# Short reads ahead of the loads, a re-scheduled head and earlier next tiles in an RMSNorm and QKV projection

## The chip, the core and the metric

The kernel runs on one core of a Trainium2 chip. The metric is the time of one execution on the device in microseconds (us); lower is better. A core has five engines with an instruction stream each: TensorE (PE, matmuls), VectorE (DVE), ScalarE (ACT), GpSimd (POOL) and SyncE (SP, which only issues transfers here). Sixteen DMA engines carry out the transfers that SP and ACT issue.

## The reference

```python
def setup_inputs():
    batch, n_heads, seq, head_dim = 8, 12, 1024, 64
    dim = n_heads * head_dim
    # x (8, 1024, 768) randn, gamma (768) ones, w_qkv (768, 2304) randn * 0.1, eps 1e-5

def reference(x, gamma, w_qkv, eps):
    rms = np.sqrt(np.mean(x ** 2, axis=-1, keepdims=True) + eps)
    x_norm = x / rms * gamma
    return np.matmul(x_norm, w_qkv).astype(np.float32)
```

There are 8,192 rows of 768 numbers. Each row is divided by its root mean square, scaled by gamma and multiplied with a 768 x 2304 matrix.

## The kernel before, in words

Rows are taken in 64 tiles of 128. A tile x_t is loaded as f32 (384 KB), cast to bf16 and transposed to xT, so that its 768 columns stand in 6 K blocks of 128 along the partitions. The weights are multiplied by gamma and converted to bf16 once (`conv`), into w_b, and stay on the chip. A tile's output has column groups at 0, 512, 1024, 1536 (512 wide) and 2048 (256 wide). Each group is six matmuls, one for each K block, into one PSUM bank (`mm`, L216). The row's factor 1/rms is applied when the bank is emptied (`evac`, L230 on DVE, L232 on ACT). Two groups of 512 make one store of 512 KB; the last group makes one of 128 KB (L236).

Everything is put in order by hand. Each step is entered in a list with a due time, the list is sorted, and the steps are issued in that order; every engine then works through its own steps in order. The due times only order the steps; nothing waits for the clock.

The head treats the first six tiles together with the weights. The weights come in 11 pieces (`PIECES`: K blocks from and to, first column, width), and `ARRIVALS` gives the order of x tiles and pieces on SP's queue: x0 x1 x2, three weight blocks, x3, and so on. Tiles 0 to 2 are transposed on TensorE directly in f32, in two halves ("trA" and "trB", L197, copied by "cpA" and "cpB"); tiles 3 to 5 are cast first and transposed in bf16 (L183). `HEAD_PLAN` lists what each engine does: conversions of weight blocks on DVE, ACT or POOL, matmuls by tile, column and K blocks, evacuations. TensorE starts with 30 matmuls on zeros (`idle`, L265) and does 5 more after tile 2's transposes. Gamma is loaded by ACT's queue (L122) and transposed on TensorE (L247).

From tile 6 on there is a steady loop with the due time `now` of the tile's first matmul. The load of x is due 15 us before, the cast 8.5, a DMA transpose on SP's queue (`trans_dma`, L206) 7.5, the square sum (`stat`) 5 and the reciprocal 3. A tile's matmuls take 5.83 us in this list. All x loads, weight loads, stores and DMA transposes go through SP in the listed order. The framework gives DMAs eight completion semaphores in turn, and a DMA waits for the one issued eight before it.

Pools set how many buffers there are: eight for x_t, four for the bf16 cast xb, nine for xT, seven for each kind of output tile, eight PSUM banks.

Of the kernel before, what the change touches and what calls it, by code (L numbers as in the profile page):

```python
# [7 lines left out]

ARRIVALS = "xxxwwwxwwwwwxxwww"
PIECES = [(0, 1, 0, 512), (1, 2, 0, 512), (2, 3, 0, 512), (3, 4, 0, 512), (4, 5, 0, 512), (5, 6, 0, 512), (0, 3, 512, 512), (3, 6, 512, 512), (0, 6, 1024, 512), (0, 6, 1536, 512), (0, 6, 2048, 256)]

EARLY = 3


HEAD_PLAN = [
    (4.41, "trA", 0), (4.45, "stat", 0), (5.28, "trB", 0), (5.42, "cpA", 0, "DVE"),
    (5.71, "trA", 1), (5.85, "cpB", 0, "ACT"), (6.10, "recip", 0), (6.44, "stat", 2),
    (6.59, "trB", 1), (6.73, "cpA", 1, "DVE"), (6.80, "trA", 2), (7.11, "conv", 0, 0, "POOL"),  # L20
    (7.24, "trB", 2), (7.41, "cpB", 1, "DVE"), (7.77, "cpA", 2, "ACT"),
    (7.81, "conv", 1, 1, "DVE"), (8.02, "mm", 0, 0, "0"), (8.23, "mm", 1, 0, "0"),
    (8.29, "recip", 2), (8.39, "cpB", 2, "ACT"), (8.45, "conv", 2, 2, "DVE"),
    (8.45, "mm", 2, 0, "0"), (8.66, "mm", 0, 0, "1"), (8.75, "stat", 1), (8.88, "mm", 1, 0, "1"),
    (9.10, "mm", 2, 0, "1"), (9.31, "mm", 0, 0, "2"), (9.44, "cast", 3, "DVE"),
    (9.53, "mm", 1, 0, "2"), (9.74, "mm", 2, 0, "2"), (10.05, "tr", 3), (10.08, "stat", 3),
    (10.11, "conv", 3, 3, "DVE"), (10.59, "recip", 1), (10.65, "mm", 0, 0, "3"),
    (10.78, "conv", 4, 4, "DVE"), (10.87, "mm", 1, 0, "3"), (11.09, "mm", 2, 0, "3"),
    (11.26, "cp", 3, "DVE"), (11.32, "mm", 0, 0, "4"), (11.45, "conv", 5, 5, "ACT"),
    (11.54, "mm", 1, 0, "4"), (11.76, "mm", 2, 0, "4"), (11.82, "recip", 3),  # L30
    (11.97, "mm", 3, 0, "01234"), (13.05, "mm", 0, 0, "5"), (13.27, "mm", 1, 0, "5"),
    (13.47, "conv", 6, 0, "DVE"), (13.47, "conv", 6, 1, "ACT"), (13.47, "conv", 6, 2, "POOL"),
    (13.48, "mm", 2, 0, "5"), (13.70, "mm", 3, 0, "5"), (13.95, "evac", 2, 0, "DVE"),
    (14.01, "mm", 0, 512, "0"), (14.18, "evac", 0, 0, "ACT"), (14.22, "mm", 1, 512, "0"),
    (14.44, "mm", 0, 512, "12"), (14.70, "evac", 1, 0, "DVE"), (14.87, "evac", 3, 0, "ACT"),
    (14.87, "mm", 1, 512, "12"), (15.30, "mm", 2, 512, "012"), (15.48, "conv", 7, 4, "DVE"),
    (15.48, "conv", 7, 5, "POOL"), (15.95, "mm", 3, 512, "012"), (16.33, "conv", 7, 3, "POOL"),
    (16.47, "cast", 4, "DVE"), (16.47, "stat", 4), (16.60, "mm", 0, 512, "45"),
    (17.03, "mm", 1, 512, "4"), (17.24, "tr", 4), (17.47, "cast", 5, "DVE"),
    (17.58, "mm", 0, 512, "3"), (17.79, "mm", 1, 512, "35"), (17.80, "stat", 5),  # L40
    (18.02, "cp", 4, "DVE"), (18.23, "tr", 5), (18.56, "mm", 2, 512, "345"), (18.58, "recip", 4),
    (18.74, "evac", 1, 512, "DVE"), (19.13, "evac", 0, 512, "ACT"), (19.21, "mm", 3, 512, "345"),
    (19.49, "evac", 2, 512, "DVE"), (19.86, "mm", 4, 0, "012345"), (20.02, "evac", 3, 512, "ACT"),
    (20.24, "recip", 5), (20.40, "cp", 5, "DVE"), (21.15, "mm", 4, 512, "012345"),
    (21.49, "conv", 8, 2, "DVE"), (21.49, "conv", 8, 3, "ACT"), (21.97, "conv", 8, 0, "DVE"),
    (22.20, "conv", 8, 4, "ACT"), (22.45, "mm", 5, 0, "012345"), (22.45, "evac", 4, 0, "DVE"),
    (22.91, "evac", 4, 512, "ACT"), (23.60, "conv", 8, 1, "ACT"), (23.74, "mm", 5, 512, "012345"),
    (23.90, "evac", 5, 0, "DVE"), (24.31, "conv", 8, 5, "ACT"), (25.04, "mm", 0, 1024, "012345"),
    (25.20, "evac", 5, 512, "DVE"), (25.51, "conv", 9, 0, "POOL"), (25.51, "conv", 9, 1, "ACT"),
    (25.95, "conv", 9, 5, "DVE"), (26.33, "mm", 1, 1024, "012345"), (26.43, "conv", 9, 4, "DVE"),  # L50
    (26.49, "evac", 0, 1024, "ACT"), (26.91, "conv", 9, 2, "DVE"), (27.39, "conv", 9, 3, "DVE"),
    (27.63, "mm", 2, 1024, "012345"), (27.87, "evac", 1, 1024, "DVE"),
    (27.90, "conv", 10, 0, "POOL"), (27.90, "conv", 10, 2, "ACT"), (28.38, "conv", 10, 3, "ACT"),
    (28.62, "conv", 10, 5, "DVE"), (28.86, "conv", 10, 4, "ACT"), (28.92, "conv", 10, 1, "DVE"),
    (28.92, "mm", 3, 1024, "012345"), (29.22, "evac", 2, 1024, "DVE"),
    (30.22, "mm", 4, 1024, "012345"), (30.38, "evac", 3, 1024, "DVE"),
    (31.51, "mm", 5, 1024, "012345"), (31.67, "evac", 4, 1024, "DVE"),
    (32.81, "mm", 0, 1536, "012345"), (32.97, "evac", 5, 1024, "DVE"),
    (34.10, "mm", 1, 1536, "012345"), (34.26, "evac", 0, 1536, "DVE"),
    (35.39, "mm", 2, 1536, "012345"), (35.55, "evac", 1, 1536, "DVE"),  # L60
    (36.69, "mm", 3, 1536, "012345"), (36.85, "evac", 2, 1536, "DVE"),
    (37.98, "mm", 4, 1536, "012345"), (38.14, "evac", 3, 1536, "DVE"),
    (39.28, "mm", 5, 1536, "012345"), (39.44, "evac", 4, 1536, "DVE"),
    (40.57, "mm", 0, 2048, "012345"), (40.73, "evac", 5, 1536, "DVE"),
    (41.23, "mm", 1, 2048, "012345"), (41.39, "evac", 0, 2048, "ACT"),
    (41.88, "mm", 2, 2048, "012345"), (42.04, "evac", 1, 2048, "DVE"),
    (42.54, "mm", 3, 2048, "012345"), (42.70, "evac", 2, 2048, "DVE"),
    (43.19, "mm", 4, 2048, "012345"), (43.35, "evac", 3, 2048, "DVE"),
    (43.85, "mm", 5, 2048, "012345"), (44.01, "evac", 4, 2048, "DVE"),
    (44.67, "evac", 5, 2048, "DVE"),  # L70
]
HEAD_END = 44.51


@with_exitstack
def kernel(
# [8 lines left out]
    nc = tc.nc  # L85
    f32 = mybir.dt.float32
# [4 lines left out]
    xf = x.flatten_outer_dims()  # L91
    of = out.flatten_outer_dims()
    M, K = xf.shape
# [3 lines left out]
    KO = K // P  # L97
    MT = M // P
    NT = 512
    HEAD = ARRIVALS.count("x")  # L100
    inv_k = 1.0 / float(K)
    PIECE_BUFS = {(k1 - k0, n): sum((q[1] - q[0], q[3]) == (k1 - k0, n) for q in PIECES)
                  for k0, k1, _, n in PIECES}

    PARTS = [(0, 1024), (1024, 1024), (2048, N - 2048)]

    singles = ctx.enter_context(tc.tile_pool(name="singles", bufs=1))
    wst = ctx.enter_context(tc.tile_pool(name="wst", bufs=3))
    xin = ctx.enter_context(tc.tile_pool(name="xin", bufs=8))
    stats = ctx.enter_context(tc.tile_pool(name="stats", bufs=12))  # L110
    junk = ctx.enter_context(tc.tile_pool(name="junk", bufs=2))
    xbp = ctx.enter_context(tc.tile_pool(name="xbp", bufs=4))
    xTp = ctx.enter_context(tc.tile_pool(name="xTp", bufs=HEAD + 3))
    outp = ctx.enter_context(tc.tile_pool(name="outp", bufs=7))
    psum = ctx.enter_context(tc.tile_pool(name="psum", bufs=8, space=bass.MemoryType.PSUM))

# [1 line left out]

    warm = singles.tile([P, P], bf16)
    nc.vector.memset(warm, 0.0)  # L120
    g6 = singles.tile([KO, P], f32)
    nc.scalar.dma_start(out=g6, in_=gamma.rearrange("(ko p) -> ko p", p=P))  # L122
    eps_sb = singles.tile([P, 1], f32)
# [77 lines left out]
            XT[t] = xTp.tile([P, KO, P], bf16, name="xT")  # L201
        copy(eng, XT[t][:, slice(*HALF[h]), :], PT[t, h])

    def trans_dma(t):
        XT[t] = xTp.tile([P, KO, P], bf16, name="xT")
        nc.sync.dma_start_transpose(out=XT[t], in_=XB[t])  # L206

    begun = {}

# [32 lines left out]
    def at(time, fn, *args):  # L242
        plan.append((time, len(plan), fn, args))
# [8 lines left out]
    def evac_at(time, t, n0, eng, gap):  # L252
        at(time, evac, t, n0, eng)
        h = part(n0)
        nl = min(NT, N - n0)
        left[t, h] = left.get((t, h), PARTS[h][1]) - nl
        if t == MT - 1:
            at(time + gap - 0.5, store, t, h, n0, nl)
        elif left[t, h] == 0:
            at(time + gap, store, t, h, *PARTS[h])  # L260
# [4 lines left out]
            nc.tensor.matmul(out=wps, lhsT=warm, rhs=warm, start=True, stop=True)  # L265


    nx = nw = 0
    for n, kind in enumerate(ARRIVALS):
        if kind == "x":  # L270
            at(0.1 * n - 9, load_x, nx)
            nx += 1
        else:
            at(0.1 * n - 9, load_w, nw)
            nw += 1
    at(0.0, idle, 30)
    ops = {"conv": conv, "cast": cast, "stat": stat, "recip": recip, "tr": tr, "cp": cp, "mm": mm}
    for time, op, *args in HEAD_PLAN:
        if op == "evac":
            evac_at(time, *args, gap=1.0)  # L280
        elif op[-1] in "AB":
            at(time, tr_half if op[:2] == "tr" else cp_half, args[0], op[-1], *args[1:])
        else:
            if op == "mm":
                args[2] = [int(k) for k in args[2]]
            at(time, ops[op], *args)
        if op == "trA" and args[0] == 0:
            at(time + 0.1, gamma_in)
        if op == "trB" and args[0] == EARLY - 1:
            at(time + 0.1, idle, 5)  # L290


    US = 6 * 0.2158 / 512
    now, flip = HEAD_END, 0
    for t in range(HEAD, MT):
        at(now - 15, load_x, t)
        at(now - 8.5, cast, t)
        at(now - 7.5, trans_dma, t)
        at(now - 5, stat, t)
        at(now - 3, recip, t)  # L300
        for n0 in range(0, N, NT):
            at(now, mm, t, n0, range(KO))
            now += min(NT, N - n0) * US
            flip ^= 1
            evac_at(now + 0.2, t, n0, "DVE" if flip else "ACT", gap=1.2)
# [38 lines left out]
```

## Time and profile before

| what | value |
|---|---|
| median of 4 runs | 390.05 us (389.92 to 390.29) |
| the profiled execution's own time | 389.57 us |
| its span, first to last instruction | 387.8 us |
| first matmul of the kernel proper | 8.52 us |
| TensorE busy | 381.9 us (98%) |
| HBM read, written | 32.25 MB, 75.50 MB |
| load of an x tile, issue to landing, median | 4.3 us |
| DMA transpose, issue to landing, median | 4.4 us |

The span runs from the first to the last instruction in the profile; the time of an execution also holds what lies around it. Engines are named as above; PEld is the loading of the stationary operand, which overlaps PE. In a timeline line the first number is the start, the second the duration in us, then engine, line, operation, output and inputs, shapes and count; brackets give how long the engine had been idle and what released it. The chain of waits is followed back from the last instruction, each step to what released it. Line numbers are those of the kernel before.

### The profile page before, as it was taken

To read this page: it belongs to the slowest core of one execution; us is meant where nothing else is said; L and a number is where in the kernel's file an instruction comes from. 1 tells how busy PE (TensorE), PEld (TensorE's weight loads), DVE (VectorE), ACT (ScalarE), POOL (GpSimd) and SP (SyncE) were. 2 spreads that over 40 slices of the span, in tenths; PEclk is the share of its full clock that TensorE was granted. 3 is DMA by queue.
4 is the path that set the end of the run, shared out by engine and by line. 5 is a ranking of instruction groups with operands and counts; after the bars stand their busy time and mean duration, and the time that the engine had idled before them with its cause. 6 is when DMAs were issued, how large, how long until landed. Compare 5 with 4: busy or idle time off the path is not lost.

```text
span 387.8 us, 5539 instructions
## 1 busy us (share of the span) xinstructions
PE 381.9 (98%) x1992; PEld 194.4 (50%) x1992; DVE 159.3 (41%) x317; ACT 178.3 (46%) x359; POOL 5.9 (2%) x12
## 2 busy tenths in 40 slices
PE   7999999999999999999999999999999999999996
PEld 6444644554554554554554554554554554554553
DVE  3676634343433343433343333343334343333332
ACT  6662244444444544444534444534434535434532
POOL 1310000000000000000000000000000000000000
PEclk9999999999999999999999999999999999999999
DMA  7999999999999999999999999999999999999974
GB/s 282 393 385 350 315 353 284 369 337 288 292 341 302 299 303 299 275 350 302 285 319 297 300 314 289 315 319 299 279 329 302 290 327 284 289 333 292 311 246 189
DMA packets 87606, 119.51 MB, mean 308 GB/s; under 512 B 50710, under 2 KB 59676, under 8 KB 87580
## 3 DMA queue, kind: packets, MB, share of 16 engines
q1 hardware_dynamic: 87568, 119.17, 100.8%
q8 instruction: 15, 0.25, 0.3%
q14 instruction: 11, 0.09, 0.1%
q10 hardware_dynamic: 12, 0.00, 0.0%
HBM read 32.25 MB, written 75.50 MB: 278 GB/s over the span
## 4 chain that ended last, share of the span: by engine, by line
PE 95%; DMA 3%; SPq 1%; DVE 0%; issue 0%; ACT 0%
PE pm L216 94%; DMA w_f<-in_w_qkv_dram 2%; DMA xT<-xb 1%; SPq L140 0%; SPq L145 0%; PE pm L183 0%; DVE w_b L151 0%; ACT ot L232 0%; DVE ot L230 0%
## 5 line engine op out<-in xcount | busy, mean ns | idle before, releaser
L216 PE MATMUL pm<-w_b,xT 128*128 128x512 bf16 (+1 forms) x1920 | 374.5, 358 | 1.3 <-POOL w_b L155 1.0
L216 PEld LDWEIGHTS <-xT 128*128 128x128 bf16 x1920 | 187.6, 98 | 187.1 <-issue 1.5
L230 DVE TENSOR_SCALAR ot<-pm,rstd 128x512 f32<-128x512 f32 (+1 forms) x168 | 116.9, 697 | 211.5 <-PE pm L216 211.4
L232 ACT ACTIVATE ot<-pm,rstd 128x512 f32<-128x512 f32 (+1 forms) x152 | 98.0, 645 | 187.3 <-PE pm L216 142.0
L170 ACT ACTIVATE sq<-x_t 128x768 bf16<-128x768 f32 x64 | 53.4, 835 | 10.0 <-DMA x_t<-in_x_dram 10.0
L159 DVE CAST xb<-x_t 128x768 bf16<-128x768 f32 x61 | 33.1, 543 | 3.6 <-DMA x_t<-in_x_dram 3.6
L172 ACT ACTIVATE rms<-ssq,eps_sb 128x1 f32<-128x1 f32 x64 | 18.9, 295 | 2.1
L170 ACT ACTIVATION_READ_ACCUMULATOR sq<-x_t 128x1 f32 x64 | 12.3, 192 | 0.0
L177 DVE RECIPROCAL rstd<-rms 128x1 f32<-128x1 f32 x64 | 9.8, 153 | 0.0
L153 ACT ACTIVATE w_b<-w_f,g_sb 128x512 bf16<-128x512 f32 (+1 forms) x10 | 6.1, 651 | 5.3 <-DMA w_f<-in_w_qkv_dram 5.3
L151 DVE TENSOR_SCALAR w_b<-w_f,g_sb 128x512 bf16<-128x512 f32 (+1 forms) x14 | 6.5, 494 | 4.9 <-DMA w_f<-in_w_qkv_dram 4.6
L155 POOL TENSOR_SCALAR w_b<-w_f,g_sb 128x512 bf16<-128x512 f32 (+1 forms) x6 | 5.2, 867 | 23.0 <-DMA w_f<-in_w_qkv_dram 23.0
L265 PE MATMUL pm<-warm 128*128 128x128 bf16 x35 | 3.8, 300 | 1.0 <-DVE eps_sb L124 1.0
L265 PEld LDWEIGHTS <-warm 128*128 128x128 bf16 x35 | 3.5, 142 | 1.0 <-DVE eps_sb L124 1.0
L197 PE MATMUL pm<-ident_f,x_t 128*128 128x128 f32 x18 | 3.0, 309 | 0.0
L197 PEld LDWEIGHTS pm<-ident_f,x_t 128*128 128x128 f32 x18 | 2.2, 158 | 0.3 <-DMA x_t<-in_x_dram 0.3
L127 ACT ACT_TABLE_LOAD x1 | 1.3, 1283 | 1.3 <-PEq L325 1.3
L248 DVE COPY g_sb<-pm 128x6 f32<-128x6 f32 x1 | 0.2, 166 | 3.8 <-PE pm L247 3.8
L159 DVE CAST xT<-pm 128x512 bf16<-128x512 f32 (+1 forms) x3 | 1.7, 596 | 0.0
L159 DVE COPY xT<-pm 128x768 bf16<-128x768 bf16 x3 | 1.6, 547 | 0.0
L183 PEld LDWEIGHTS <-xb 128*128 128x128 bf16 x18 | 1.2, 98 | 0.9 <-DVE xb L159 0.4
L183 PE MATMUL pm<-ident,xb 128*128 128x128 bf16 x18 | 1.5, 220 | 0.0
(13 smaller groups left out, 3.1 us busy)
## 6 DMA issues: line engine op xcount, KB each, us to landing
out_dram<-ot SPq DMA_DIRECT2D x126, 512.0 KB, 3.9
x_t<-in_x_dram SPq DMA_DIRECT2D x64, 384.0 KB, 4.3
out_dram<-ot SPq DMA_DIRECT2D x64, 128.0 KB, 3.2
w_f<-in_w_qkv_dram SPq DMA_DIRECT2D x2, 1536.0 KB, 12.7
w_f<-in_w_qkv_dram SPq DMA_DIRECT2D x3, 768.0 KB, 8.4
w_f<-in_w_qkv_dram SPq DMA_DIRECT2D x6, 256.0 KB, 5.9
out_dram<-ot SPq DMA_DIRECT2D x4, 256.0 KB, 2.0
xT<-xb SPq DMA_TRANSPOSE x58, 4.4
```

Of the source, the lines that this page charges most:

```text
L151: nc.vector.tensor_scalar(out=o, in0=i, scalar1=g, scalar2=None, op0=mult)
L153: nc.scalar.activation(out=o, in_=i, func=AF.Copy, scale=g, bias=0.0)
L155: nc.gpsimd.tensor_scalar(out=o, in0=i, scalar1=g, scalar2=1.0, op0=mult, op1=mult)
L159: nc.vector.tensor_copy(out=out, in_=in_)
L170: nc.scalar.activation(out=sq, in_=X[t], func=AF.Square, accum_out=ssq)
L172: nc.scalar.activation(out=rms, in_=ssq, func=AF.Sqrt, scale=inv_k, bias=eps_sb)
L177: nc.vector.reciprocal(out=r, in_=RS[t])
L197: nc.tensor.transpose(out=PT[t, h][:, ko - k0, :], in_=X[t][:, ko * P:(ko + 1) * P], identity=ident_f)
L216: nc.tensor.matmul(out=PM[t, n0][:, :nl], lhsT=XT[t][:, ko, :], rhs=w_b[:, ko, n0:n0 + nl], start=(b == 1), stop=(b == KO))
L230: nc.vector.tensor_scalar(out=o, in0=pm[:, :nl], scalar1=RS[t], scalar2=None, op0=mult)
L232: nc.scalar.activation(out=o, in_=pm[:, :nl], func=AF.Copy, scale=RS[t], bias=0.0)
L265: nc.tensor.matmul(out=wps, lhsT=warm, rhs=warm, start=True, stop=True)
```

## The change

Two more loads are put at the front of ACT's queue, ahead of gamma. Each reads 16 numbers (64 bytes) from every eighth row, 96 places in all: one over the 768 rows of the weights, one over the first 768 rows of x, which are tiles 0 to 5. Nothing uses what they load.

The weight pieces are cut anew. The first has two K blocks (512 KB), then come four of one block, three of two blocks for columns 512 to 1023, and the three large ones as before. The loads stand in an explicit list `LOADS`: first the two-block piece, then x0, x1, x2, a weight block, x3, three more blocks, the three two-block pieces, x4, the columns from 1024, those from 1536, x5, those from 2048, x6 and x7. x6 and x7 were issued by the steady loop before, behind the first stores; now they stand ahead of all stores.

`HEAD_PLAN` is a new list. Its first matmuls take K blocks 0 and 1 of tile 0, ahead of the transposes of tile 2. Columns from 1024 on begin after five tiles, and tile 5's matmuls come late: its columns 0 to 2047 run just before the last group of all tiles. The idle matmuls are 25 at the start and 10 after gamma's transpose, which now comes ahead of x0's.

In the steady loop the load, the cast and the DMA transpose of tiles 6 to 10 are due 6 us earlier. There are two more buffers for x_t, xb and xT each.

```diff
-ARRIVALS = "xxxwwwxwwwwwxxwww"
-PIECES = [(0, 1, 0, 512), (1, 2, 0, 512), ..., (0, 3, 512, 512), (3, 6, 512, 512), (0, 6, 1024, 512), (0, 6, 1536, 512), (0, 6, 2048, 256)]
+HEAD = 6
+PIECES = [(0, 2, 0, 512), (2, 3, 0, 512), (3, 4, 0, 512), (4, 5, 0, 512), (5, 6, 0, 512), (0, 2,
+          512, 512), (2, 4, 512, 512), (4, 6, 512, 512), (0, 6, 1024, 512), (0, 6, 1536, 512), (0,
+          6, 2048, 256)]
+LOADS = [
+    (-9.00, "w", 0), (-8.99, "x", 0), (-8.98, "x", 1), (-8.97, "x", 2), (-8.96, "w", 1),
+    (-8.95, "x", 3), (-8.94, "w", 2), (-8.93, "w", 3), (-8.92, "w", 4), (-8.91, "w", 5),
+    (-8.90, "w", 6), (-8.89, "w", 7), (-8.88, "x", 4), (-8.87, "w", 8), (-8.86, "w", 9),
+    (-8.85, "x", 5), (-8.84, "w", 10), (-8.83, "x", 6), (-8.82, "x", 7),
+]
 HEAD_PLAN = [
...
+    (4.75, "conv", 0, 0, "POOL"), (4.75, "conv", 0, 1, "DVE"), (5.30, "trA", 0),
...
+    (6.99, "recip", 0), (7.04, "trB", 1), (7.15, "cpB", 0, "DVE"), (7.18, "cpA", 1, "ACT"),
+    (7.26, "mm", 0, 0, "01"), (7.55, "cpB", 1, "DVE"), (7.69, "trA", 2),
...
+    (20.05, "conv", 8, 3, "DVE"), (20.25, "mm", 4, 512, "012345"), (20.53, "evac", 4, 0, "DVE"),
+    (20.76, "conv", 8, 5, "ACT"), (21.00, "conv", 8, 2, "POOL"), (21.28, "conv", 8, 4, "DVE"),
+    (21.55, "mm", 0, 1024, "013245"), (21.71, "evac", 4, 512, "ACT"),
...
-HEAD_END = 44.51
+HEAD_END = 43.94
-    xin = ctx.enter_context(tc.tile_pool(name="xin", bufs=8))
+    xin = ctx.enter_context(tc.tile_pool(name="xin", bufs=10))
-    xbp = ctx.enter_context(tc.tile_pool(name="xbp", bufs=4))
-    xTp = ctx.enter_context(tc.tile_pool(name="xTp", bufs=HEAD + 3))
+    xbp = ctx.enter_context(tc.tile_pool(name="xbp", bufs=6))
+    xTp = ctx.enter_context(tc.tile_pool(name="xTp", bufs=HEAD + 5))
+    touch = singles.tile([16, 2, KO, 16], f32)
+    for i, a in enumerate((w_qkv, xf[:K])):
+        nc.scalar.dma_start(out=touch[:, i], in_=a.rearrange("(t p e) n -> p t e n", p=16, e=8)[:, :, 0, :16])
     g6 = singles.tile([KO, P], f32)
     nc.scalar.dma_start(out=g6, in_=gamma.rearrange("(ko p) -> ko p", p=P))
...
-    at(0.0, idle, 30)
+    for time, kind, n in LOADS:
+        at(time, {"x": load_x, "w": load_w}[kind], n)
+    at(0.0, idle, 25)
+    at(3.6, gamma_in)
+    at(3.61, idle, 10)
...
-            evac_at(time, *args, gap=1.0)
+            evac_at(time, *args, gap=max(1.0, LOADS[-1][0] + 0.1 - time))
...
     for t in range(HEAD, MT):
-        at(now - 15, load_x, t)
-        at(now - 8.5, cast, t)
-        at(now - 7.5, trans_dma, t)
+        ahead = 6.0 if t < HEAD + 5 else 0.0
+        if ("x", t) not in {q[1:] for q in LOADS}:
+            at(now - 15 - ahead, load_x, t)
+        at(now - 8.5 - ahead, cast, t)
+        at(now - 7.5 - ahead, xbar, t, nc.sync)
         at(now - 5, stat, t)
```

## The prediction

> **What bounds the kernel now.** I read the page first: engines, then the chain that ended last.
>
> ```profile
> PE 381.9 (98%) x1992; PEld 194.4 (50%) x1992; DVE 159.3 (41%) x317; ACT 178.3 (46%) x359; POOL 5.9 (2%) x12
> PEclk9999999999999999999999999999999999999999
> ```
>
> TensorE is busy for 98% of the span at its full granted clock, so time can come only from stretches in which it does something other than the kernel's own matmuls. The chain in order of time says where those stretches are:
>
> ```profile
> 4.02 6.58 DMA w_f<-in_w_qkv_dram
> 11.17 6.80 PE pm L216 x30
> 19.32 25.96 PE pm L216 x138
> 45.52 5.76 DMA xT<-xb
> 51.33 332.89 PE pm L216 x1710
> ```
>
> From 51.33 to 384.22 us there are 57 tiles of 27 units (a unit is one 512-wide matmul; a 256-wide one is half). 332.89 / 1539 is 0.2163 us a unit, so this stretch has no gap, and whatever the change does to the start of tile 7 (51.33) it does to the end. Seven tiles before that are 189 units, 40.88 us; the other 10.45 us are the ground that can be won or lost. Of these 8.52 lie before the first matmul, and 0.39 before tile 7: tile 6 starts at 45.10, 27 units end at 50.94, and tile 7 waits until 51.33 for its DMA transpose.
>
> The timeline shows when the loads arrive, by the first instruction that waited for each:
>
> ```profile
> 4.02 0.84 ACT L170 ACTIVATE sq<-x_t 128x768 bf16<-128x768 f32 x1 [1.18 <-DMA x_t<-in_x_dram]
> 6.38 0.84 ACT L170 ACTIVATE sq<-x_t 128x768 bf16<-128x768 f32 x1 [0.27 <-DMA x_t<-in_x_dram]
> 7.78 0.69 POOL L155 TENSOR_SCALAR w_b<-w_f,g_sb 128x512 bf16<-128x512 f32 x1 [6.47 <-DMA w_f<-in_w_qkv_dram]
> 8.52 2.10 PE L216 MATMUL pm<-w_b,xT 128*128 128x512 bf16 x9 [0.97 <-POOL w_b L155]
> 9.95 0.56 DVE L159 CAST xb<-x_t 128x768 bf16<-128x768 f32 x1 [0.49 <-DMA x_t<-in_x_dram]
> 10.62 0.49 DVE L151 TENSOR_SCALAR w_b<-w_f,g_sb 128x512 bf16<-128x512 f32 x1
> 16.09 2.04 POOL L155 TENSOR_SCALAR w_b<-w_f,g_sb 128x512 bf16<-128x512 f32 x2 [1.03 <-DMA w_f<-in_w_qkv_dram]
> 22.67 1.33 ACT L153 ACTIVATE w_b<-w_f,g_sb 128x512 bf16<-128x512 f32 x2 [1.33 <-DMA w_f<-in_w_qkv_dram]
> ```
>
> Tile x0 is there at 4.02, x2 at 6.38, the first weights at 7.78, x3 at 9.95 and the fourth weight block 0.67 later. 256 KB in 0.67 and (8.97 to 9.95) 384 KB in 0.98 are 391 KB a us. At that pace the 1,536 KB from x0 to the third weight block would have taken 3.93; they came at 8.97, 4.95 later. About 1.02 us of arrivals are lost between 4 and 8 us. The windows show the place (columns: busy times, granted clock, DMA share, GB/s):
>
> ```profile
> 3.00:4.00 1.00, 1.00 (x12) 1.00 (x11) 0.00 (x0) 0.00 (x0) 0.00 (x0) 1.00 1.06 421
> 5.00:6.00 1.00, 1.00 (x10) 0.88 (x9) 0.64 (x2) 0.54 (x2) 0.00 (x0) 1.00 0.89 253
> 9.00:12.00 3.00, 2.91 (x18) 1.31 (x17) 2.27 (x6) 1.75 (x6) 0.00 (x0) 1.00 1.05 394
> ```
>
> The dip to 253 GB/s comes as the first weight rows are read; the first half us of x (2.0 to 2.5) moved only 166 GB/s, while later pieces run at 394. Reading a place for the first time looks slow here.
>
> **The change part by part.** *Touches.* Two loads of 96 pieces of 64 bytes, 12 KB, go out on ACT's queue ahead of gamma. ACT is idle until x0, so its two issues (0.57 each by gamma's) are hidden. On the 16 DMA engines they are 12 packets each. A 384 KB load has 8 packets of 3,072 bytes per engine in 0.98 (0.122 each), a 256 KB one 8 of 2,048 in 0.67 (0.084); that line leaves 0.010 for 64 bytes, so 12 cost 0.12. Bounds: by bytes alone 0.03; as dear as a 3,072-byte packet, 1.47. I take 0.12, nearest to how the rows scale. What they return lies between nothing and the 1.02. I take all: the later weights lie 5 us behind them, and the load that now goes first replaces x0 in paying the start. Its own excess (0.57 at the first weights against 0.29 at x0) may stay, 0.28, inside the range.
>
> *Touches against the rules.* The Trainium skill, DMA: Bandwidth & Descriptors, section Bandwidth, calls transfers under 64 KB descriptor-dominated and times a 4 KB one at 0.68 us of DMA; no row here shows a load so small by itself. By it the two touches would cost about 1.36 (estimate), and the sum below would end near 390.5 instead of 389.2.
>
> *Load order.* Two K blocks, x0, x1, x2, then the rest. Bytes needed ahead of the first matmul fall from 1,408 to 1,280 KB (the order puts x1's transposes before it), so it goes from 8.52 to about 7.2: x1 at 4.02 + 896/391 + 0.12 = 6.43, six transposes at 0.107 (0.64), then the copy. But the columns from 1024 on are now wanted after five tiles instead of six. Tile 0's fourth matmul there (K block 2; the list has 0, 1, 3, 2) waits for the second of two POOL conversions of the 1,536 KB piece. That piece was ready at 22.67; x5 now comes after it, minus 0.98; minus 1.02 plus 0.12 by the touches: 20.79. POOL's pair takes 2.04 (row at 16.09) plus 0.11 of handovers: 22.94. TensorE itself is there at about 22.55: 7.2, plus 63 units (13.63), transposes of tiles 2, 3, 4 (0.64 + 0.68), plus 0.4 of handovers like those before (10.24 to 11.17). So the piece decides. Behind it are 99 units (21.41) and tile 5's transposes (0.34): tile 6 starts at 44.69 instead of 45.10.
>
> *Next tiles ahead of stores.* On SP x6 and x7 pass five stores, and the transposes of tiles 6 to 10 and their casts (DVE) come 6 us earlier. In the profile the transpose of tile 7 was issued at 45.52 behind stores; now it goes out near 37, behind its cast. The 0.39 wait goes. Late next would be tile 8: five 512 KB stores, three more and x8 take 6.2 + 3.7 + 1 after about 30 (stores of that kind landed 1.23 apart), so x8 lands near 42, its cast holds DVE for up to 1 us, and its transpose has until 56. The displaced stores land 2 us later; their buffers (seven) are next written at tile 7.
>
> *Waits added.* DMAs take eight semaphores in turn, so with two more at the front SP's load of x3 waits for the first touch, and the next ones for the first weights, the second touch and gamma. Behind them stand all loads; 1,920 KB are queued by then, work until about 8 us, so this is free unless a touch lands later than that. Gamma now sits behind the touches; PE waits for it, then issues ten idle matmuls (30 of them took 3.38) before x0 at about 5.4: free until gamma comes after 4.3, and 0.39 of slack behind it. More buffers, and 25 + 10 idle matmuls for 30 + 5, cost nothing.
>
> Sum: tile 7 starts at 44.69 + 5.84 = 50.53, 0.80 before 51.33. The profiled execution took 389.57 (span 387.8 and 1.8 around it), 0.48 under the median of 390.05, and the gain is taken off the median: **389.2**. About 0.2%, 0.78 us, is what a measurement of this kernel can tell from no change.
>
> **The rivals.**
> (1) The dips stay and the touches cost their 0.12. With neither, tile 6 starts at 44.69 + 1.02 - 0.12 = 45.59 and tile 7 at 51.43; 0.12 on top is 51.55, or 0.22 late: 390.3. For it: the first load has no lead over its touch, and each place is still read first by somebody. Against: the later blocks have 5 us.
> (2) The other side: a touch packet holds its DMA engine as long as a 3,072-byte one, 1.47, and the dips stay. 51.43 + 1.47 is 52.90, 1.57 late: 391.6. The start of tile 7 is level when the touches cost 0.10 less than they win, and it is slower by 0.2% once they cost 0.68 more. For it: the 0.29 lost at x0's first packets. Against: gamma's small packets beside x at 421 GB/s.
> (3) The 1,536 KB piece took 4.68 behind x5 where 3.93 was due. If that 0.75 does not return, it is not the bound, and TensorE's 22.55 counts: 0.39 more, 388.9.
> (4) TensorE stays at its slow start. In the trace warm-up matmuls and transposes run 0.107 and 0.21 apart until 5.2 us and half that from then on; with a pause for gamma the doubling may come later. If it comes at 10, the 2.8 after the first matmul lose 1.4, less 0.39 slack: 1.0, so 390.3.
> The Trainium skill, TensorE: Matmul & The Clock Gate, Part 1, ties the doubling to about 3.4 us of sustained activity. A pause would put it one such window later, near 8.6, and by the page the loss is 0.3 (estimate); the granted clock shows 1.00 throughout and cannot tell.
>
> **How the numbers follow.** Likeliest 0.45 (own range 388.9 to 389.6, from the 0.28 and the 0.03 to 0.35 a touch may cost, so it lies on both sides of 389.27; 0.28 of it faster, 0.17 same); (1) 0.19 (0.15 same, 0.04 slower); (2) 0.12, slower; (3) 0.18, faster; (4) 0.06, half same, half slower. Faster 0.46, same 0.35, slower 0.19. The range goes from 388.5, case (3) with the touches at 0.03 and shorter handovers, to 390.9, the middle of (2).
>
> **What would show it.** Right: no window under 350 GB/s between 3 and 8 us, x0 near 5.4, first matmul near 7.2, the 1,536 KB piece near 20.8, one short wait for POOL about 22.5, tile 6 at 44.7, no wait for xT. Wrong: slow windows before 5 us with touches in flight, x0 after 6, gamma after 5, or a wait for xT at tiles 8 to 11.

## The result and the profile after

The changed kernel takes 390.78 us (median of 46 runs, 389.42 to 392.04) against 389.92 us for the kernel before beside it (64 runs, 389.14 to 390.84). The ratio is 1.0024, 95% interval 1.0019 to 1.0030: slower by about 0.9 us, where 0.8 us less was predicted. The profiled execution took 390.69 with a span of 388.9; before it was 389.57 with 387.8.

The page of the kernel after, its engine line and its clock row, looks as before:

```profile
PE 382.2 (98%) x1992; PEld 195.8 (50%) x1992; DVE 159.5 (41%) x314; ACT 176.4 (45%) x356; POOL 9.1 (2%) x18
PEclk9999999999999999999999999999999999999999
```

TensorE still does the same work at the full granted clock, and the difference lies in the head. The chain of waits of the kernel after, in order of time (start, duration, what):

```profile
0.73 0.46 ACTq L137
...
1.22 0.47 ACTq L137
...
1.72 3.88 DMA g<-in_gamma_dram
...
5.73 0.24 PE pm L264
5.97 1.18 PE pm L282 x10
7.15 2.56 PE pm L214 x12
9.71 0.57 PE pm L233 x2
...
29.17 355.97 PE pm L233 x1839
```

The chain now begins with the two touches on ACT's queue (L137) and goes on with gamma, the small load behind them. Gamma is issued at 1.72 and lands at 5.60. After it come the ten idle matmuls (L282), the transposes of x0 and x1 (L214), and then TensorE's own work without a wait (the chain puts it at 9.71, the end of the transposes; the first matmul starts at 9.51). Tile 6 starts at 46.54 (45.10 before), tile 7 at 52.37 (51.33 before). The wait for tile 7's DMA transpose is gone: 52.37 is 46.54 plus 5.83. So the profiled execution loses 1.44 us up to tile 6, wins 0.39 back at tile 7, and is 1.1 longer at the end of its span.

The timeline of the kernel after shows the head's first steps:

```profile
0.98 2.85 PE L282 MATMUL pm<-warm 128*128 128x128 bf16 x25 [0.98 <-DVE eps_sb L141]
5.73 0.24 PE L264 MATMUL pm<-ident_f,g 6*128 6x6 f32 x1 [1.90 <-DMA g<-in_gamma_dram]
5.88 0.84 ACT L187 ACTIVATE sq<-x_t 128x768 bf16<-128x768 f32 x1 [2.04 <-DMA x_t<-in_x_dram]
5.91 1.25 PE L282 MATMUL pm<-warm 128*128 128x128 bf16 x10
6.95 2.77 PE L214 MATMUL pm<-ident_f,x_t 128*128 128x128 f32 x12
9.51 0.78 PE L233 MATMUL pm<-w_b,xT 128*128 128x512 bf16 x2
21.73 1.36 POOL L172 TENSOR_SCALAR w_b<-w_f,g_sb 128x512 bf16<-128x512 f32 x2 [6.07 <-DMA w_f<-in_w_qkv_dram]
```

Three things cost time here. First, TensorE stands idle for 1.90 us until gamma is there. Second, x0 has been there since 5.86, but TensorE then does ten idle matmuls and reaches x0 only at 6.95. Third, it does all this at its early pace: the ten idle matmuls are 0.11 us apart and the twelve transposes 0.21, where the later pace is half of that. The first matmul starts at 9.51 instead of 8.52. POOL's pair for the 1,536 KB piece, which was to set the end, runs at 21.73 and no instruction of TensorE waits for it.

The windows of the kernel after (busy times, granted clock, DMA share, GB/s) show the arrivals:

```profile
2.00:2.50 0.50, 0.50 (x8) 0.50 (x6) 0.00 (x0) 0.16 (x1) 0.00 (x0) 1.00 0.45 72
2.50:3.00 0.50, 0.50 (x8) 0.50 (x6) 0.00 (x0) 0.50 (x1) 0.00 (x0) 1.00 1.01 268
3.00:4.00 1.00, 0.83 (x8) 0.56 (x6) 0.00 (x0) 0.82 (x2) 0.00 (x0) 1.00 0.95 348
4.00:5.00 1.00, 0.00 (x0) 0.00 (x0) 0.00 (x0) 0.00 (x0) 0.00 (x0) 1.00 1.07 414
5.00:6.00 1.00, 0.27 (x3) 0.28 (x4) 0.00 (x0) 0.12 (x1) 0.00 (x0) 1.00 1.03 402
```

The dip to 253 GB/s at 5 to 6 us is gone, but the start has become slower: 72 and 268 GB/s where the kernel before had 166 and 370. The slow stretch is at the front now; it has not vanished. The six profiles of the new order without touches, further down, have it there too (71 to 128 GB/s at 2 to 2.5 us), and 326 to 399 GB/s at 5 to 6 us. So it is the new order that moved it, and not the touches. The first 1,920 KB (x0, x1, x2 and three weight blocks in both kernels) are complete at 8.49 instead of 8.95.

### The profile page after: what moved, and what is told of

Same layout as the page of the kernel before. It is cut to its first block, busy times and chain, and to the rows that moved or that the text cites. A ratio compares the mean times of both kernels' runs of the same rounds, so it can differ in the third digit from the quotient of the medians.

```text
span 388.9 us, 5539 instructions
## 1 busy us (share of the span) xinstructions
PE 382.2 (98%) x1992; PEld 195.8 (50%) x1992; DVE 159.5 (41%) x314; ACT 176.4 (45%) x356; POOL 9.1 (2%) x18
## 4 chain that ended last, share of the span: by engine, by line
PE 98%; DMA 1%; ACTq 0%; ACT 0%; issue 0%
PE pm L233 96%; DMA g<-in_gamma_dram 1%; PE pm L214 1%; PE pm L282 0%; PE pm L200 0%; ACTq L137 0%; ACT ot L249 0%; PE pm L264 0%
## 5 line engine op out<-in xcount | busy, mean ns | idle before, releaser
L172 POOL TENSOR_SCALAR w_b<-w_f,g_sb 128x512 bf16<-128x512 f32 (+1 forms) x12 | 8.4, 711 | 20.2 <-DMA w_f<-in_w_qkv_dram 15.3
L168 DVE TENSOR_SCALAR w_b<-w_f,g_sb 128x512 bf16<-128x512 f32 (+1 forms) x9 | 5.4, 602 | 0.0
L282 PE MATMUL pm<-warm 128*128 128x128 bf16 x35 | 4.1, 312 | 1.0 <-DVE eps_sb L141 1.0
L282 PEld LDWEIGHTS <-warm 128*128 128x128 bf16 x35 | 3.6, 146 | 1.0 <-DVE eps_sb L141 1.0
L214 PE MATMUL pm<-ident_f,x_t 128*128 128x128 f32 x18 | 3.8, 372 | 0.0
L214 PEld LDWEIGHTS pm<-ident_f,x_t 128*128 128x128 f32 x18 | 3.3, 200 | 0.5 <-PE pm L214 0.2
L178 ACT CAST xT<-pm 128x512 bf16<-128x512 f32 (+1 forms) x2 | 0.9, 468 | 2.2 <-PE pm L214 2.2
```

The source lines that it names most:

```text
L168: nc.vector.tensor_scalar(out=o, in0=i, scalar1=g, scalar2=None, op0=mult)
L172: nc.gpsimd.tensor_scalar(out=o, in0=i, scalar1=g, scalar2=1.0, op0=mult, op1=mult)
L214: nc.tensor.transpose(out=PT[t, h][:, ko - k0, :], in_=X[t][:, ko * P:(ko + 1) * P], identity=ident_f)
```

## The experiments

The ratio of each run is to the kernel before on the same chip (35 runs of it each time). The same kernel gave 0.9997 and 0.9983 on two chips, and the quotient of two medians differs from the ratio by up to 0.0011 (the run with gamma's load first). Differences of ratios below about 0.0015 between chips are therefore not read. Profiles are single executions, and their times are given where they differ from the median.

**Gamma's load ahead of the touches.**

```diff
+    g6 = singles.tile([KO, P], f32)
+    nc.scalar.dma_start(out=g6, in_=gamma.rearrange("(ko p) -> ko p", p=P))
     touch = singles.tile([16, 2, KO, 16], f32)
     for i, a in enumerate((w_qkv, xf[:K])):
         nc.scalar.dma_start(out=touch[:, i], in_=...)
-    g6 = singles.tile([KO, P], f32)
-    nc.scalar.dma_start(out=g6, in_=gamma.rearrange("(ko p) -> ko p", p=P))
```

> The changed kernel with gamma's load put back at the front of ACT's queue, the two touches behind it; all else as changed. Theory A (gamma's lateness is the loss: in the changed kernel gamma's packets move at 4.6 to 5.0 us, TensorE idles from 3.6 to 5.73 and then runs its warm-ups and transposes at the slow pace until about 10): gamma lands before 3.5, TensorE warms up as before, first matmul near 7.6, tile 7 near 50.8, ratio to the kernel before about 0.9985. Theory B (the loads themselves are late, x0 at 5.86 and the 1,536 KB piece at 21.64, because the touches hold them up): the first matmul moves, but tile 7 stays near 52 and the ratio near 1.002.

Measured: 389.86 us, 1.0001 (0.9992 to 1.0010). The loss against before is gone, but the 0.9985 of theory A did not come either. Timeline of TensorE in this kernel:

```profile
3.77 0.27 PE L264 MATMUL pm<-ident_f,g 6*128 6x6 f32 x1
3.97 1.25 PE L282 MATMUL pm<-warm 128*128 128x128 bf16 x10
5.71 2.82 PE L214 MATMUL pm<-ident_f,x_t 128*128 128x128 f32 x12 [0.49 <-DMA x_t<-in_x_dram]
8.32 0.63 PE L233 MATMUL pm<-w_b,xT 128*128 128x512 bf16 x1
```

Gamma is transposed at 3.77 instead of 5.73, x0's transposes start when x0 is there, and the first matmul comes at 8.32 instead of 9.51. The transposes are still 0.21 apart, although the only pause is one of 0.5 us before x0. So gamma's place costs about 1.2 us at the first matmul in these two profiles, and the slow pace does not need gamma's long pause.

**No touches.**

```diff
-    touch = singles.tile([16, 2, KO, 16], f32)
-    for i, a in enumerate((w_qkv, xf[:K])):
-        nc.scalar.dma_start(out=touch[:, i], in_=...)
```

> The changed kernel without the two touches, so gamma is alone on ACT's queue. Theory A: gamma comes early, TensorE is warm, but the dips of the weights' first rows come back: x0 near 5.9, weight blocks 0.3 to 0.5 later than with touches, first matmul near 8.0, ratio about 1.000. Theory B: the loads start earlier without touches, x0 near 5.4, and the ratio is below 0.999, better than with gamma first.

Measured: 389.28 us, 0.9977 (0.9968 to 0.9986), 0.58 us under the run with gamma first. The profiled execution (389.89) was one of this kernel's longest; most lie at 389.1 to 389.3. In it the pace doubles early and the first matmul starts at 7.73, the first 1,920 KB are complete at 8.62, and a new wait appears. The ratio is the one of theory B, but its reason is not seen: x0 landed at 5.66 us here and at 5.67 with gamma first. The chain of waits:

```profile
9.62 12.67 DMA w_f<-in_w_qkv_dram
...
22.38 0.99 POOL w_b L169
23.41 4.78 PE pm L230 x21
```

This is a wait for the piece that the prediction named as its bound, though not at the place it named. The piece landed at 22.29, and the first of POOL's two conversions, K block 0, ends at 23.37. TensorE stands from 22.24 to 23.41 ahead of the group's first matmul, while the prediction let it wait ahead of the fourth, for POOL's second conversion. The head cannot use all that the faster start wins.

**Touches and late gamma kept, TensorE kept busy until then.**

```diff
-    at(0.0, idle, 25)
+    at(0.0, idle, 44)
```

> The changed kernel with 44 idle matmuls instead of 25 ahead of gamma's transpose, so that TensorE is busy until gamma lands; gamma stays behind the touches. Theory A with the clock as the larger part: the pace doubles near 5.2 as in the kernel before, the ten idle matmuls and the transposes take half, first matmul near 8.1, ratio about 0.9995. If only the wait for gamma counts and not the pace: first matmul near 9.3, ratio about 1.002. Theory B: ratio 1.002.

Measured: 389.73 us, 0.9991 (0.9982 to 1.0000). Timeline of TensorE in this kernel:

```profile
0.99 4.87 PE L282 MATMUL pm<-warm 128*128 128x128 bf16 x44 [0.99 <-DVE eps_sb L141]
5.82 0.24 PE L264 MATMUL pm<-ident_f,g 6*128 6x6 f32 x1
5.99 0.74 PE L282 MATMUL pm<-warm 128*128 128x128 bf16 x10
6.57 1.48 PE L214 MATMUL pm<-ident_f,x_t 128*128 128x128 f32 x12
7.96 0.39 PE L233 MATMUL pm<-w_b,xT 128*128 128x512 bf16 x1
```

Gamma's transpose is as late as in the changed kernel (5.82), yet the twelve transposes take 1.48 instead of 2.77, and the first matmul starts at 7.96 instead of 9.51. All transfers are those of the changed kernel; only TensorE's pause was filled. By the ratios this is worth 0.0033, or 1.3 us. So the late gamma alone is not the whole loss: the pause that it makes puts off the doubling of the pace. In this profile tile x4 came 1.1 us later than in the changed kernel's (17.68 against 16.55), and TensorE stood for 0.8 us before its transposes; that takes part of the gain.

**The touches alone, in the kernel before, behind gamma.**

```diff
     nc.scalar.dma_start(out=g6, in_=gamma.rearrange("(ko p) -> ko p", p=P))
+    touch = singles.tile([16, 2, KO, 16], f32)
+    for i, a in enumerate((w_qkv, xf[:K])):
+        nc.scalar.dma_start(out=touch[:, i], in_=...)
```

> The kernel before with the two touches added behind gamma, and nothing else of the change. If the touches take the dips away at little cost: x2 and the weight blocks 0.4 to 0.6 earlier, first matmul near 8.0, but tile 7 may still wait for its transpose, whose place in SP's queue is unchanged; ratio 0.9985 to 1.000. If the touches cost what they win (theory B): the blocks come at the same time as before and the ratio is 1.000 or above.

Measured: 390.86 us, 1.0027 (1.0011 to 1.0044), runs from 389.70 to 392.82. The touches by themselves make the old order slower. The profiled execution, at 392.73 among the longest of these runs, begins its chain with them:

```profile
1.71 6.75 DMA touch<-in_x_dram
8.47 0.33 SPq L148
...
9.32 7.71 DMA w_f<-in_w_qkv_dram
```

The touch over x landed at 8.46, and SP stood for it with the next weight load until 8.47. The arrivals did not get smoother either. Windows of the same kernel:

```profile
4.00:5.00 1.00, 0.99 (x10) 0.72 (x7) 0.06 (x1) 0.95 (x3) 0.00 (x0) 1.00 1.02 290
5.00:6.00 1.00, 0.96 (x8) 0.67 (x7) 0.99 (x4) 0.65 (x2) 0.00 (x0) 1.00 0.91 232
6.00:7.00 1.00, 0.00 (x0) 0.00 (x0) 0.81 (x2) 0.00 (x0) 0.00 (x0) 1.00 0.93 308
```

The kernel before had 363, 253 and 356 there, and its x2 landed at 6.36 instead of 8.10. In this profile touches that run among the loads return nothing of the dip. This execution is 1.9 us over the median, so its profile shows how far it can go, not the usual size.

**No touches and a fuller warm-up; gamma first with the same warm-up.** These two differ in the touches alone.

```diff
-    touch = ...                      # first kernel: no touches
-    at(3.61, idle, 10)
+    at(3.61, idle, 17)               # both kernels; the second: gamma's load first, touches behind it
```

> The changed kernel without the touches and with 17 idle matmuls instead of 10 behind gamma's transpose, so that TensorE has no pause from 0.98 us until x0 at about 5.7. Theory P (the pace doubles only after a stretch of some 3.4 us without a pause, and where this falls differs from run to run): the doubling comes by 7.8 at the latest in every run; ratio 0.9975 or below, runs within 0.5 us of each other but for strays. Theory Q (the pace has no part, gamma's lateness and the touches' cost to the loads are all): the ratio is that of the changed kernel without touches, 0.998, with no smaller spread.

> The same with the two touches behind gamma. Theory P: gamma first (ratio 1.0001 with a pause of 0.8 us ahead of x0) was slow because the pause fell into the stretch; without it the first matmul comes near 7.7 and the ratio is at or below that without touches, since with touches the 1,536 KB piece came 0.4 to 0.6 earlier in the profiles (21.7 against 22.3): 0.9965 to 0.9975. Theory Q: touches cost the loads and the ratio stays near 1.000.

Measured on one chip: 389.74 us, 0.9997 (0.9987 to 1.0007) without touches, and 390.32 us, 1.0013 (1.0000 to 1.0025) with them. Again the touches cost 0.58 us. Seven more idle matmuls brought nothing that can be read, and the ratios of theory P (0.9975 or below, and 0.9965 to 0.9975) did not come. The first matmul starts at 7.77 and 7.76, so in these profiles the touches do not act before it, and an early first matmul alone does not make the kernel faster; in the second, the chain goes through tile x4:

```profile
8.69 9.38 DMA x_t<-in_x_dram
...
18.10 0.57 DVE xb L176
...
18.72 0.51 PE pm L200 x6
```

TensorE has nothing to do from 17.43 to 18.72. The same wait appears without touches in two other profiles below, so it is not theirs.

**A short warm-up in the kernel before.** This tests the pace by itself.

```diff
-    at(0.0, idle, 30)
+    at(0.0, idle, 10)
```

> The kernel before with 10 idle matmuls instead of 30 at the start, so that TensorE pauses from about 2.1 us until x0 at 4.1; nothing else is changed, and all loads keep their times. Theory P: the doubling slips from 4.4 to 7.8 to at least 7.5, transposes ahead of the first matmul take 0.107 longer each (up to 1.9 in all), the first matmul comes near 9, some matmuls run at half pace; ratio 1.001 to 1.004 and a wide spread of runs, 1.5 us or more. Theory Q: the loads decide, ratio 1.000.

Measured: 390.38 us, 1.0004 (0.9993 to 1.0014): nothing that can be told from no change, and less than theory P's 1.001 to 1.004. TensorE idles 1.77 us before x0, and its next 14 transposes take 2.74 instead of 2.02, but the first matmul starts at 8.63 instead of 8.52, since there it waits for the weights in either case. In the order before the pace of the transposes has cover; in the new order, in which the weights come first, it has none.

**The later tiles by the loop again.** The kernel without touches and with the fuller warm-up, but x6 and x7 and the casts and transposes of tiles 6 to 10 not ahead of the stores.

```diff
-    (-8.85, "x", 5), (-8.84, "w", 10), (-8.83, "x", 6), (-8.82, "x", 7),
+    (-8.85, "x", 5), (-8.84, "w", 10),
-        ahead = 6.0 if t < HEAD + 5 else 0.0
+        ahead = 0.0
```

> The changed kernel without touches, with 17 idle matmuls, and without the earlier next tiles: x6 and x7 are loaded by the steady loop and nothing of tiles 6 to 10 is due earlier. If the earlier next tiles take away the wait of tile 7 (0.39 us in the kernel before), this one waits there again, for longer since its head ends earlier: 0.4 to 1.0 us slower than the same with earlier tiles, ratio 0.9985 to 1.000. If they bring nothing, the two ratios are the same.

Measured: 389.78 us, 0.9995 (0.9986 to 1.0004), the same as 389.74 with them. x6 and x7 land at 36.3 and 43.1 instead of 29.8 and 30.8, and no tile waits for its transpose. So tile 7's wait did not go because its load passed the stores. What is left of the change there is two more buffers for x_t, xb and xT each and the shifted list; which of them removed the wait was not tried.

**Everything as changed, but gamma's transpose behind x0's.**

```diff
-    (4.75, "conv", 0, 0, "POOL"), (4.75, "conv", 0, 1, "DVE"), (5.30, "trA", 0),
+    (5.45, "conv", 0, 0, "POOL"), (5.45, "conv", 0, 1, "DVE"), (5.30, "trA", 0),
-    at(3.6, gamma_in)
+    at(5.4, gamma_in)
```

> The changed kernel with every transfer as changed (touches first, gamma behind them), but gamma's transpose on TensorE and the first two conversions behind x0's first four transposes, so that TensorE does not stand before x0 and waits for gamma beside work. Theory G (in the changed kernel the loss is TensorE standing from 3.6 to 5.73 for gamma, and the slow pace that follows until about 10): all 35 idle matmuls run through to 4.8, x0's transposes start near 5.9, first matmul near 7.8 to 8.4 instead of 9.51; ratio near that of gamma first, 1.000 to 1.001, against 1.0024. Theory B (the loads are late): ratio stays at 1.002 or more.

Measured: 389.75 us, 0.9984 (0.9974 to 0.9995). Touches and gamma are issued in the changed kernel's order; TensorE alone no longer stands for gamma in its warm-up. Timeline of this kernel, whose profiled execution took 390.17:

```profile
0.99 3.92 PE L282 MATMUL pm<-warm 128*128 128x128 bf16 x35 [0.99 <-DVE eps_sb L141]
5.87 1.09 PE L214 MATMUL pm<-ident_f,x_t 128*128 128x128 f32 x4 [0.97 <-DMA x_t<-in_x_dram]
6.89 0.27 PE L264 MATMUL pm<-ident_f,g 6*128 6x6 f32 x1
7.09 1.97 PE L214 MATMUL pm<-ident_f,x_t 128*128 128x128 f32 x8
8.85 0.63 PE L233 MATMUL pm<-w_b,xT 128*128 128x512 bf16 x1
```

The 35 idle matmuls run through, x0 is taken at 5.87 when it lands, and the first matmul starts 0.66 earlier than in the changed kernel although the pace is still slow here. By medians the gain is 1.0 us, by the ratios 0.0040 or 1.6 us; the profile, 0.42 over its median, shows 0.66 of it. The ratio is below theory G's 1.000 to 1.001 and the first matmul later than its 7.8 to 8.4, so the first matmul does not account for the whole gain. The result puts the loss on TensorE's place in line behind gamma, with all transfers left as they were; two conversions moved with the transpose, and the ten idle matmuls now fill part of the pause.

**No touches and a fuller warm-up once more, on this chip.** The code is that of the earlier run.

> The kernel of nt_warm once more (no touches, 17 idle matmuls), as the base of the next two on the same chip. Ratio 0.998 to 1.000. Theory F (one 16 KB read of instructions holds one DMA engine for 1.1 us; in the new order x4 and the 1,536 KB piece come just when TensorE wants them, so wherever that read falls it costs up to 1.5): two groups of runs, near 389.2 and near 389.75, and a profile of a run of the later group shows x4 near 17.9 and TensorE waiting for its cast.

Measured: 389.47 us, 0.9983 (0.9974 to 0.9992). Its ratio equals the 0.9984 of the run above, which has the touches; the medians are 0.28 us apart. So the touches cost little or nothing here once TensorE doesn't stand for gamma, where the other two pairs showed 0.58 us; but this pair differs in more than the touches. What the touches cost beyond gamma stays open between nothing and 0.6 us. In this profile x4 lands at 17.85 and TensorE waits from 17.15 to 18.50. The two groups of runs that theory F expected do not show: the runs lie evenly from 389.09 to 389.94.

**More slack for tile 4.** As the run before, with tile 4's transposes placed behind more matmuls.

```diff
-    (16.68, "tr", 4), (17.01, "mm", 3, 512, "3"), (17.23, "mm", 0, 512, "45"),
-    (17.41, "recip", 4), (17.57, "cp", 4, "DVE"), (17.66, "mm", 1, 512, "45"),
+    (18.08, "tr", 4), (17.01, "mm", 3, 512, "3"), (17.23, "mm", 0, 512, "45"),
+    (18.10, "recip", 4), (18.11, "cp", 4, "DVE"), (17.66, "mm", 1, 512, "45"),
```

> nt_warm with tile 4's transposes moved behind the matmuls of tiles 0 and 1 on K blocks 4 and 5 at column 512, so that x4 has about 1.4 us more. Theory F: where nt_warm waits about 1.5 for x4, this one waits little, but TensorE then comes to the 1,536 KB piece earlier and waits there up to 0.6 to 1.4 (seen without touches); 0.2 to 0.5 us faster than nt_warm. If x4's lateness is not what costs: no difference.

Measured: 389.32 us, 0.9976 (0.9967 to 0.9985). The wait for x4 is gone and the next one takes its place:

```profile
10.06 12.04 DMA w_f<-in_w_qkv_dram
...
22.18 1.00 POOL w_b L169
23.22 4.78 PE pm L230 x21
```

That is the 1,536 KB piece again: TensorE stands for 0.55 us, until 23.22. The gain over the run before, 0.15 us by medians, cannot be told from nothing.

**The 1,536 KB piece cut in two as well.** The halves have three K blocks each; the K order and the conversions follow.

```diff
-          512, 512), (2, 4, 512, 512), (4, 6, 512, 512), (0, 6, 1024, 512), (0, 6, 1536, 512), ...
+          512, 512), (2, 4, 512, 512), (4, 6, 512, 512), (0, 3, 1024, 512), (3, 6, 1024, 512),
+          (0, 6, 1536, 512), ...
-    (20.05, "conv", 8, 3, "DVE"), ... (21.55, "mm", 0, 1024, "013245"),
+    (20.54, "conv", 9, 3, "DVE"), ... (21.55, "mm", 0, 1024, "012345"),
```

> x4_slack with the 1,536 KB piece cut into two of 768 KB (K blocks 0 to 2 and 3 to 5), so that the columns from 1024 can begin 2 us earlier, K blocks in order. Theory F: no wait of TensorE longer than 0.5 us between the first matmul (7.8) and tile 6, which starts near 45.0; ratio 0.996 to 0.9975, faster than both kernels. If the arrivals do not decide: the same as x4_slack.

Measured: 389.26 us, 0.9979 (0.9970 to 0.9988). The halves land at 19.52 and 21.55, and nothing waits at 22 us. Timeline of TensorE:

```profile
19.02 8.15 PE L230 MATMUL pm<-w_b,xT 128*128 128x512 bf16 x37
27.31 0.51 PE L197 MATMUL pm<-ident,xb 128*128 128x128 bf16 x6
```

Its next wait is 0.3 us until 27.31, for x5. This version beats the changed kernel and the one before (0.8 us by the ratio), but not the run before it, and its ratio is a little above the 0.9975 that was expected at most. In these three profiles each wait that is removed shows a shorter one behind it (1.35, 0.55 and 0.3 us), and the time hardly moves. All versions whose interval lies below 1 leave the touches out or take gamma out of TensorE's way.

## Why the prediction was wrong, and where it was right

**The step that failed** is the one on added waits: gamma behind the touches is "free until gamma comes after 4.3, and 0.39 of slack behind it". Gamma came at 5.60; "gamma after 5" was one of the signs of being wrong. The price of a touch packet was right: the packet records show 8 to 11 ns each, against the 10 used, so 0.12 us for the twelve of one DMA engine. (The 1.36 us that the prediction set beside this is not what the engines spent; that the 390.5 from it lies near the result is chance. A load as small by itself, which the prediction said no row shows, is in the kernel before too: gamma, 3 KB in six packets of 25 to 41 ns.) But the 192 packets of 64 bytes moved from 1.84 to 4.85 us, 3.0 us for twelve packets an engine, a mean of 0.25 each. Meanwhile the engines served the loads on SP's queue. The kernel after, 3 to 4 us (queue, packets, MB, share of the 16 engines; q1 is SP's queue, q10 ACT's; both rows also count packets of 4 bytes):

```profile
q1 hardware_dynamic: 171, 0.34, 90.8%
q10 hardware_dynamic: 70, 0.00, 4.6%
```

Gamma's packets moved at 4.58 to 4.97, behind most of the touches'. The sum priced what the touches take from the loads, and had no term for how long they close ACT's queue; gamma's time stood there only as a condition, taken as met. These are two quantities, and the second was 25 times the first. With nothing ahead of them gamma's six packets move at 1.7 to 2.6 in the kernel before and at 1.7 to 1.8 in the run with gamma first.

The Trainium skill, DMA: Bandwidth & Descriptors, section Queues, rings and completion order, says that a DMA engine goes round robin between the queues that it has work for, a packet at a time. The landings here agree in kind: touches at 3.92 and 5.36, gamma at 5.60. The size does not follow from it. Taking turns with one packet of a load (0.084 or 0.122 us by the prediction's rows), twelve touch packets would take 1.1 to 1.6 us (an estimate), but over the 3.0 us the packet records have 373 packets of the loads to the 192 of the touches, about two to one. In the runs with 44 idle matmuls and with gamma's transpose behind x0's, no touch packet started between 2.83 and 3.59 us, between the last one of the first touch and the first one of the second. Why it is more than a turn for each packet is not shown.

**From there the loss ran through a rival.** The fourth, the pace doubled late because of a pause for gamma, had 0.06 of the chances and a price of 1.0 us. In the changed kernel's profile the pace doubles at about 10 us, as that rival had supposed. The first matmul came at 9.51 against the predicted 7.2, 2.31 late. Its parts: x1 landed at 6.84 instead of 6.43, 0.4; x0's transposes started 1.1 after x0 landed, because of gamma and the ten idle matmuls; and the twelve transposes took 1.3 longer than at the later pace. These overlap by about half a microsecond. Filling the pause (0.9991 against 1.0024) and moving gamma's transpose (0.9984) each take the loss away; they support that the pause and the place in line are its cause. How much belongs to the pace and how much to the standing is not split, since the time of the doubling differs between executions.

**The gain from the touches was mis-sized.** They were to return all 1.02 us of dips. In the profiles of the new order the first 1,920 KB are complete at 8.40 to 9.05 without touches (mean 8.68 over six profiles) and at 8.35 to 8.76 with them (mean 8.58 over five). So of the 0.37 that the new order with touches wins on 8.95, about 0.1 goes with the touches, which is less than the spread within either group; the rest is the order itself. With and without touches the slow windows stand at 2 to 3 us, and in the old order the touches left the dip where it was (232 GB/s at 5 to 6). That is nearer to the first rival, by which the dips stay. Its reason, that each place is still read first by somebody, was not tested.

**The 1,536 KB piece** landed at 21.64 in the changed kernel, against 20.8 predicted, and was not the bound there, because TensorE came later. Where TensorE came on time it was: the runs without touches and with slack for x4 stand for 1.17 and 0.55 us at 22 us. The prediction had one short wait there, but for K block 2, POOL's second conversion; the runs wait for K block 0, the first, because the piece landed at 22.29 and 22.09. POOL's pair took 1.36 after the piece, not 2.04.

**Right:** tile 7's wait for its transpose went, and no wait for xT at tiles 8 to 11 came in its place; but the earlier tiles were not the reason, as the loop's own order does as well. SP's waits for the touches were free in the changed kernel: the loads of x3 and of the fourth weight piece were held until 3.94 and 5.37, with the arrivals still back to back. In the old order SP stood for a touch until 8.47, so this is not free in general.

**The forecast** of 389.2 missed by 1.6 us; tile 6 was put at 44.69 and started at 46.54, 1.85 late: the 2.31 at the first matmul, less the 0.39 of slack that it used up, is 1.92. The pace of 391 KB a us is 388 by the prediction's own rows (640 KB in 1.65 us), which moves none of its terms by more than 0.04. 390.78 lies inside the range, near its upper end, though the range reached there by another mechanism, the second rival's dear touch packets.

## What to carry to other kernels

A small transfer has two costs: what it takes from the others, which is its bytes and packets, and how long the queue behind it is closed, which beside busy DMA engines was 25 times as long here. What the start needs at once, like gamma here, goes ahead of what nobody waits for. And a pause made in TensorE's warm-up has to be priced at the slow pace for all that follows until the doubling, unless something else covers it.

## What the runs showed of the hardware

- **Small packets wait their turn.** 192 packets of 64 bytes, twelve for each engine, took 3.0 us beside the loads in the changed kernel (1.8 to 4.5 in the five other profiles with touches), at 8 to 11 ns of work each. The landing of the x touch varied from 4.9 to 8.5 us after the start over the runs.
- **The doubling of TensorE's pace varies between executions:** 3.7 us (touches in the old order), 4.2 (no touches), about 5.2 (before), 6 (44 idle matmuls), 7.2 (short warm-up) and 9.7 to 9.9 (gamma's transpose later, gamma first, changed). The same code, without touches and with the fuller warm-up, gave 4.0 in one profile and 5.7 to 6.0 in the other. The granted clock in the windows shows 1.00 in all of them, so it has to be read from the spacing of the transposes (0.107 or 0.21). The Trainium skill, TensorE: Matmul & The Clock Gate, Part 1, describes an activity window of about 3.4 us that runs free of the kernel's start. The variation between executions agrees with it. So does the run with gamma first, where TensorE is at work from 0.99 but for short pauses and still slow at 9: counted back from the doubling at 9.8 in steps of 3.4 us (an estimate with the page's figure), one window runs from 6.4 to 9.8 and the one before it from 3.0 to 6.4, and the pause ahead of x0 falls into that one. How long a pause must be to spoil a window was not measured.
- **An instruction read may delay a load.** In the profiles one read of 16 KB on the instruction queue, a single packet, takes 1.0 to 1.1 us of a DMA engine. Where it falls between 14.1 and 15.9 us, in six profiles of the new order, x4 lands about 1.1 later in four (17.7 to 18.1, against 16.4 to 17.1 in all others), and TensorE, which has no slack there in the new order, waits 0.8 to 1.4. This is a coincidence over profiles, not a shown cause.
